# Layer one's gate and MLP scale by packed TensorE rows, its MLP shift by VectorE dot products, the input weights' low parts on VectorE

## The chip, the cores and the metric

One core of one Trainium2 chip runs the whole program. TensorE (PE) multiplies matrices into PSUM, VectorE (DVE), ScalarE (ACT) and GpSimd (POOL) work on tiles, and SyncE (SP) issues nearly all transfers. The metric is device time of one execution in microseconds (us); the program is one launch.

## The reference

A two-layer generator: each layer turns a conditioning vector into six modulation vectors of 1024 (shift, scale and gate of the mixer, then shift, scale and gate of the MLP), for latent tokens (512) and context tokens (256) apart.

```python
for l in range(DEPTH):
    mx = jnp.split((silu_c @ w_mod[l] + b_mod[l])[:, None, :], N_MOD, axis=-1)
    mc = jnp.split(silu_cc @ w_mod[l] + b_mod[l], N_MOD, axis=-1)
    zx = modulate(rms_norm(x, norm1_g[l]), mx[0], mx[1]) @ w_in[l]
    zc = modulate(rms_norm(ctx, norm1_g[l]), mc[0], mc[1]) @ w_in[l]
    ...                                        # Fourier, latent attention, convolution
    x = x + mx[2] * mixer_rest(fx, gx, attn_x, l)
    hx = modulate(rms_norm(x, norm2_g[l]), mx[3], mx[4])
    x = x + mx[5] * channel_mlp(hx, l)
return rms_norm(x, final_norm_g)
```

What matters here is where the 6144 modulation columns of layer one (l = 0 in the code) are made, and when each is needed: mx[0] and mx[1] at once, mx[2] (the gate, columns 16 to 23 of the tile mod, 128 values to a column) at the output projection, mx[3] and mx[4] (columns 24 to 39) at the norm before the MLP.

## The kernel before

Activations lie transposed: features on the 128 partitions, tokens along the row. Every product is made in three passes (mm3): a float32 operand is split into a rounded high part and a low part that is the rest, and high x high, high x low and low x high are summed in PSUM. load_w does it for weights: SP loads 512 KB into a tile raw, ScalarE writes the high part, and the engine named by eng (GpSimd by default) subtracts it from raw for the low part.

In start, the input projection of layer one runs over eight blocks of 128 features. For each, load_win loads 896 columns of weights (tiles wk and hl, L152 the low part), and put_h makes the activations: VectorE scales (L345), ScalarE adds the shift and rounds (L346), VectorE makes the low part (L347). Shift and scale come from TensorE in four pieces: load_mod loads 512 columns of the modulation weights (four tiles mq), mod_rows multiplies them, eight matmuls whose stationary tile c32 has only 32 columns and which stand in four column groups of the array (tile_position, L324), and mod_cols turns the rows into columns with a small selection matrix sel4. sq_ctx sums the squares of the context tokens: ScalarE squares, GpSimd adds (L353).

In mixer, a convolution on VectorE (L747) and a Fourier part lead to attention, a loop over 48 units of a head and 128 queries. From its thirteenth unit on, every sixth puts one of four gate pieces into the background: gate_columns loads 256 columns (gw, 1 MB), multiplies them with cpp, which has two columns, and turns the result.

Then the output projection: eight blocks of weights wo, each 48 matmuls (the last two 24 at first, the context's 24 later), and behind each update adds the product into the residual on VectorE (L990) and squares it (ScalarE) into a sum for the norm. mod_group makes one column of mod by VectorE dot products (L270): it loads 128 transposed columns (mw, 512 KB) and multiplies and sums over 1024, once for latent and once for context. Sixteen columns, 24 to 39, are made here, behind the first blocks. At the end set_a and norm_chain start the MLP's norm (L216, L220, L221), and first_pairs splits the first MLP weights (hs, L1054 and L1055).

The order in which instructions stand on each engine is made by a scheduler from the program's order; each engine then runs its own list in that order, and SP's list is also the order of the loads. The scheduler also decides which buffer of a pool a load takes.

```python
wo_mods = [24, 32, 25, 33, 26, 34, 27, 35, 28, 36, 29, 37, 30, 38, 31, 39]
...
            for _ in range(3 if m < NW else 1):
                if wo_mods:
                    w = mwp.tile([P, D], F32, tag="mw", name=nm("mw"), bufs=4)
                    mod_group(mods, w, 0, wo_mods.pop(0))
```

## Time and profile before

| | us |
|---|---|
| median of 3 runs | 1632.77 |
| lowest, highest | 1628.58, 1635.89 |
| the profiled execution | 1634.36 |
| its span | 1632.6 |

| engine | busy us | share of the span |
|---|---|---|
| PE | 1520.0 | 93% |
| DVE | 1233.2 | 76% |
| ACT | 698.3 | 43% |
| POOL | 689.1 | 42% |

The program runs through stages with different limits, so these shares say little of one stage. Three stages hold what the change touches: the input projection (0 to 100 us), attention (about 165 to 352) and the output projection (about 352 to 430). The rest, the MLP of layer one and all of layer two, is issued in the same order before and after. In the rows below a line that begins with a start and a length names the engine behind them; in square brackets stands how long the engine was idle before and what ended that.

### The profile page before, as it was taken

What the parts mean: (1) busy time and instruction counts of PE and PEld (TensorE: products, weight loads), DVE (VectorE), ACT (ScalarE), POOL (GpSimd) and SP (SyncE); (2) the same over time, 40 slices, a digit from 0 to 9 for tenths busy, and PEclk for the clock granted to TensorE, in tenths of its full rate; (3) what the DMA queues carried; (4) which work ended last, traced back from release to release, by engine and by line L of the source; (5) the groups of instructions that cost most, each with busy time, mean ns of one, the idle gap of its engine ahead of it and who ended that gap; (6) DMA issues with size and microseconds to landing.
All of it is one profiled execution on the core that took longest, in us unless ns stands there. A gap on an engine that the chain in (4) does not pass through costs nothing.

```text
span 1632.6 us, 24752 instructions
## 1 busy us (share of the span) xinstructions
PE 1520.0 (93%) x9508; PEld 1329.1 (81%) x9508; DVE 1233.2 (76%) x1984; ACT 698.3 (43%) x1291; POOL 689.1 (42%) x455
## 2 busy tenths in 40 slices
PE   5898999999899999999999999899999979999997
PEld 3598877787788988889999988777878778889897
DVE  3379687779999799987887768978866676566655
ACT  3343577651432333323332244258954434444442
POOL 1415233213135455534444333343325566666671
PEclk9999999999899999999999999999999989999998
DMA  8321102147142333333433332100123122233322
GB/s 282 117 98 57 36 21 86 37 154 250 61 168 67 107 112 117 104 129 125 148 117 105 127 104 99 46 26 8 53 65 117 52 85 91 84 102 104 104 78 65
DMA packets 50567, 159.55 MB, mean 98 GB/s; under 512 B 5745, under 2 KB 13713, under 8 KB 49425
## 3 DMA queue, kind: packets, MB, share of 16 engines
q1 hardware_dynamic: 50016, 152.69, 28.6%
q0 software_dynamic: 432, 5.28, 0.8%
q8 instruction: 75, 1.23, 0.3%
q14 instruction: 44, 0.35, 0.1%
HBM read 155.84 MB, written 2.11 MB: 97 GB/s over the span
## 4 chain that ended last, share of the span: by engine, by line
PE 44%; DVE 30%; DMA 9%; issue 8%; ACT 6%; POOL 3%; SPq 0%; DVEq 0%; ACTq 0%; POOLq 0%
PE ps L156 23%; PE pv L156 10%; DVE mj L270 7%; DMA acc<-in_wmodT 7%; PE tr L156 5%; DVE aw L747 3%; DVE resx L990 2%; PE tr L865 2%; PE po L156 1%; ACT p L849 1%; PE p L156 1%; DVE t L1168 1%; DMA raw<-in_w 1%; DVE resc L990 1%; DVE t L1138 1%
## 5 line engine op out<-in xcount | busy, mean ns | idle before, releaser
L156 PE MATMUL ps<-y,hl 128*128 128x512 f32 (+1 forms) x2004 | 411.2, 358 | 13.0 <-DVE resc L990 4.7
L156 PEld LDWEIGHTS ps<-y,hl 128*128 128x128 f32 x2004 | 328.0, 190 | 74.3 <-DVE resc L990 8.8
L152 POOL TENSOR_TENSOR hl<-raw,hl 128x1024 fp32r<-128x1024 f32 (+2 forms) x92 | 229.8, 2500 | 271.1 <-ACT hl L151 263.1
L156 PE MATMUL pv<-y,hl 128*128 128x512 f32 (+1 forms) x1032 | 212.8, 356 | 5.7 <-POOL hl L152 2.7
L156 PEld LDWEIGHTS pv<-y,hl 128*128 128x128 f32 x1032 | 168.6, 189 | 37.4 <-POOL hl L152 3.2
L151 ACT ACTIVATE hl<-raw 128x1024 fp32r<-128x1024 f32 (+2 forms) x94 | 98.1, 1044 | 226.4 <-PE pv L156 112.0
L1055 POOL TENSOR_TENSOR hs<-raw,hs 128x512 fp32r<-128x512 f32 x95 | 133.2, 1404 | 125.6 <-ACT hs L1054 125.6
L156 PE MATMUL ps<-h,hs 128*128 128x256 f32 (+1 forms) x1080 | 151.2, 292 | 5.3 <-DVE t L1210 3.2
L156 PEld LDWEIGHTS ps<-h,hs 128*128 128x128 f32 x1080 | 140.1, 192 | 11.4 <-issue 3.6
L1054 ACT ACTIVATE hs<-raw 128x512 fp32r<-128x512 f32 x133 | 83.0, 629 | 146.8 <-PE tr L156 30.0
L270 DVE CUSTOM_DVE_ANT_0 mj<-acc,cb,vec 128x1024 bf16<-128x1024 f32 x64 | 103.1, 1611 | 39.7 <-DMA acc<-in_wmodT 39.7
L990 DVE SCALAR_TENSOR_TENSOR resx<-ps,mod,resx 128x512 f32<-128x512 f32 (+1 forms) x134 | 95.7, 719 | 40.2 <-PE ps L156 40.1
L1162 POOL TENSOR_TENSOR y<-t,y 128x256 fp32r<-128x256 f32 (+1 forms) x78 | 73.7, 959 | 120.2 <-DVE t L1168 112.8
L156 PE MATMUL tr<-h,hs 128*128 128x256 f32 x624 | 83.3, 283 | 0.0
L869 DVE TENSOR_TENSOR pT<-tr,pT 128x384 fp32r<-128x384 f32 (+1 forms) x144 | 74.1, 534 | 10.0 <-ACT pT L868 9.4
L868 ACT ACTIVATE pT<-tr 128x384 fp32r<-128x384 f32 (+1 forms) x144 | 65.9, 477 | 32.7 <-PE tr L865 31.7
L156 PE MATMUL pv<-h,hs 128*128 128x256 f32 (+1 forms) x504 | 77.2, 303 | 2.2 <-DVE h L221 2.2
L156 PEld LDWEIGHTS tr<-h,hs 128*128 128x128 f32 x624 | 78.5, 191 | 0.6
L865 PE MATMUL tr<-ident,p 128*128 128x128 f32 x416 | 68.7, 279 | 9.6 <-DVE pT L869 6.8
L156 PEld LDWEIGHTS pv<-h,hs 128*128 128x128 f32 x504 | 69.4, 194 | 5.9 <-DVE h L221 2.6
L156 PE MATMUL po<-pT,v 128*128 128x256 f32 x416 | 72.4, 298 | 1.3 <-DVE t L894 1.1
L1167 ACT ACTIVATE t<-t 128x256 f32<-128x256 f32 (+1 forms) x52 | 32.7, 629 | 93.7 <-DVE t L1210 93.7
(291 smaller groups left out, 2962.0 us busy)
## 6 DMA issues: line engine op xcount, KB each, us to landing
raw<-in_w SPq DMA_DIRECT2D x128, 512.0 KB, 3.7
acc<-in_wmodT SPq DMA_DIRECT2D x48, 512.0 KB, 3.5
raw<-in_wo SPq DMA_DIRECT2D x17, 512.0 KB, 4.3
mq<-in_wmods SPq DMA_DIRECT2D x16, 512.0 KB, 7.9
mw<-in_wmodT SPq DMA_DIRECT2D x16, 512.0 KB, 4.3
ztab<-in_dftx POOLq DMA_DIRECT2D x2, 2064.0 KB, 9.4
gw<-in_wmodg SPq DMA_DIRECT2D x4, 1024.0 KB, 4.9
y<-in_wmodT SPq DMA_DIRECT2D x8, 512.0 KB, 5.4
```

Of the source, the lines that this page charges most:

```text
L151: SC.activation(w[:, 0], raw, AF.Copy)
L152: side[eng].tensor_tensor(w[:, 1], raw, f(w[:, 0]), ALU.subtract)
L156: PE.matmul(o, lhsT=l, rhs=r, start=start, stop=stop)
L270: V.tensor_tensor_reduce(j, w, c[:, v], 1.0, vc("bmod", l, g), ALU.mult, ALU.add, mod[l][v][:, g:g + 1])
L747: V.scalar_tensor_tensor(acw[ct], us[ct][:, i:i + wide], vc("wdw", l, ct * TAPS + i), acw[ct], ALU.mult, ALU.add)
L865: PE.transpose(tr[:, (kt - ka) * P:(kt - ka + 1) * P], ptiles[i][:, kt * P:kt * P + P], ident)
L868: SC.activation(d[:, 0], src, AF.Copy)
L869: V.tensor_tensor(d[:, 1], src, f(d[:, 0]), ALU.subtract)
L990: mark[0] = V.scalar_tensor_tensor(r, pt[:, a - o0:b - o0], mod[l][v][:, gate * 8 + m:gate * 8 + m + 1], r, ALU.mult, ALU.add).ins
L1054: SC.activation(w[:, 0], src, AF.Copy)
L1055: side[eng].tensor_tensor(w[:, 1], src, f(w[:, 0]), ALU.subtract)
L1162: GP.tensor_tensor(ht[:, 1, a:a + n], src, f(ht[:, 0, a:a + n]), ALU.subtract)
```

## The change

The helpers load_mod, mod_rows and mod_cols move out of start and serve three places. The array wmods holds ten pieces of 512 columns instead of four; wmodg, with the gate's four pieces of 256, is gone. The gate (pieces 4 and 5) is made in attention and the MLP's scale (pieces 8 and 9) in the output projection, by packed TensorE rows; the MLP's shift (columns 24 to 31) stays with VectorE's dot products, now spread over the blocks by a table. load_win asks for the low parts on VectorE, and sq_ctx adds its squares there too. c32 and sel4 become constants of the whole program. Bytes loaded stay the same.

```diff
+    c32 = cst.tile([P, KT, 32], F32, name="c32")
+    sel4 = cst.tile([P, 2], F32, name="sel4")
...
+    def load_mod(q, pl, bufs):
+        ws = [pl.tile([P, 2, 512], F32, tag="mq", name=nm("mq"), bufs=bufs) for _ in range(4)]
+        for i, w in enumerate(ws):
+            SY.dma_start(w, A["wmods"][q, :, 2 * i:2 * i + 2])
+        return ws
+
+    def mod_rows(ws, pl, bufs):
+        pt = pst()
+        for k in range(KT):
+            g = 32 * (k % 4)
+            PE.matmul(pt[g:g + 32, :], lhsT=c32[:, k], rhs=ws[k // 2][:, k % 2], start=k < 4, stop=k >= 4,
+                      tile_position=(0, g))
+        r = pl.tile([P, 512], F32, tag="mr", name=nm("mr"), bufs=bufs)
+        SC.activation(r, pt, AF.Copy)
+        return r
+
+    def mod_cols(q, row):
+        pt = pst()
+        for i in range(4):
+            mm(pt[:, 2 * i:2 * i + 2], row[:, i * P:(i + 1) * P], sel4, True, True)
+        for v in range(2):
+            if q >= 4:
+                o = slice(4 * q, 4 * q + 4)
+                V.tensor_tensor(mod[0][v][:, o], pt[:, v:8:2], vc("bmod", 0)[:, o], ALU.add)
+                continue
...
         def load_win(k):
-            wks.append(load_w(A["win0"][k], 896, *((wk, "wk", 6) if k < 6 else ())))
+            wks.append(load_w(A["win0"][k], 896, *((wk, "wk", 6) if k < 6 else ()), eng="V"))
...
         def sq_ctx(kk):
-            sq = acc[:, S:T] if kk == 0 else tmp(C)
-            SC.activation(sq, xt[kk][:, S:T], AF.Square)
-            if kk:
-                GP.tensor_tensor(acc[:, S:T], acc[:, S:T], sq, ALU.add)
+            add_square(acc[:, S:T], xt[kk][:, S:T], kk == 0)
...
-        gp, pieces = [], list(range(4))
+        gp, pieces = [], [4, 5]
 
         def gate_columns(q):
-            w = gp[0].tile([P, KT, 256], F32, tag="gw", name=nm("gw"), bufs=1)
-            SY.dma_start(w, A["wmodg"][q])
-            yield 1
-            pt = pst()
-            for k in range(KT):
-                mm(pt[0:2, 0:256], cpp[:, k], w[:, k], k == 0, k == KT - 1)
-            rows = gp[0].tile([2, 256], F32, tag="gr", name=nm("gr"), bufs=1)
-            SC.activation(rows, pt[0:2, 0:256], AF.Copy)
-            yield 1
...
+            ws = load_mod(q, gp[0], 4)
+            yield 1
+            row = mod_rows(ws, gp[0], 1)
+            yield 1
+            mod_cols(q, row)
             yield 1
...
-        wo_mods = [24, 32, 25, 33, 26, 34, 27, 35, 28, 36, 29, 37, 30, 38, 31, 39]
+        wo_mods = {1: 8, 4: 9} if mods else {}
+        wo_dots = (2, 2, 1, 1, 1, 1, 0, 0) if mods else (0,) * KT
+        ready, dots = load_mod(8, mwp, 4) if mods else None, list(range(24, 32))
+        cols_of = []
...
-            if mods:
-                for _ in range(3 if m < NW else 1):
-                    if wo_mods:
-                        w = mwp.tile([P, D], F32, tag="mw", name=nm("mw"), bufs=4)
-                        mod_group(mods, w, 0, wo_mods.pop(0))
+            if cols_of:
+                mod_cols(*cols_of.pop())
+            if m in wo_mods:
+                q = wo_mods[m]
+                cols_of.append((q, mod_rows(ready, mwp, 2)))
+                if q < 9:
+                    ready = load_mod(q + 1, mwp, 4)
+            for _ in range(wo_dots[m]):
+                mod_group(mods, mwp.tile([P, D], F32, tag="mw", name=nm("mw"), bufs=2), 0, dots.pop(0))
```

How that moves instructions is shown at three places. The first is VectorE near the end of the input projection, where the last shift and scale columns arrive (tr_485) and the activations of the last two blocks (y) are made from x. Before:

```order
L337 TENSOR_TENSOR mod_79<-tr_485,vec 128x2 x2
L337 TENSOR_TENSOR mod_80<-tr_485,vec 128x2
L338 SCALAR_TENSOR_TENSOR av_83<-mod_79,vec 128x2
L337 TENSOR_TENSOR mod_80<-tr_485,vec 128x2
L345 SCALAR_TENSOR_TENSOR t_496<-x_122,av_83,bcs 128x512
L338 SCALAR_TENSOR_TENSOR av_84<-mod_80,vec 128x2
L345 SCALAR_TENSOR_TENSOR t_500<-x_123,av_83,bcs 128x512
L347 SCALAR_TENSOR_TENSOR y_99<-t_496,mod_79,y_99 128x512
```

After, from the row behind the first two of these columns on:

```order
L156 TENSOR_TENSOR hl_456<-raw_454,hl_456 128x896
L308 SCALAR_TENSOR_TENSOR av_85<-mod_81,vec 128x2
L306 TENSOR_TENSOR mod_82<-tr_485,vec 128x2
L352 SCALAR_TENSOR_TENSOR t_496<-x_123,av_85,bcs 128x512
L156 TENSOR_TENSOR hl_461<-raw_459,hl_461 128x896
L308 SCALAR_TENSOR_TENSOR av_86<-mod_82,vec 128x2
L354 SCALAR_TENSOR_TENSOR y_101<-t_496,mod_81,y_101 128x512
L352 SCALAR_TENSOR_TENSOR t_500<-x_124,av_85,bcs 128x512
L194 TENSOR_TENSOR sq_125<-sq_125,t_504 128x256
```

The two low parts of the weights (hl) and the additions of squares (sq) now stand between them; two more additions, the last y and one more addition follow. The first two blocks have the same form: both subtractions stand ahead of the two y.

The second is TensorE in the output projection, at the border between the second block of weights (product pv) and the third (product ps). Before:

```order
L156 MATMUL pv_3597<-y_3252,hl_3511 128x256 x2
L156 MATMUL pv_3597<-y_3252,hl_3511 128x512
L156 MATMUL pv_3597<-y_3252,hl_3511 128x256
L156 MATMUL ps_3676<-y_1360,hl_3671 128x512 x2
L156 MATMUL ps_3676<-y_1360,hl_3671 128x256 x2
L156 MATMUL ps_3676<-y_1360,hl_3671 128x512
```

After, where the rows tr are made from the four tiles of the MLP scale's first piece:

```order
L160 MATMUL pv_3580<-y_3232,hl_3491 128x512
L160 MATMUL pv_3580<-y_3232,hl_3491 128x256
L288 MATMUL tr_3637<-mq_3509,c_79 32x512 x2
L288 MATMUL tr_3637<-mq_3510,c_79 32x512 x2
L288 MATMUL tr_3637<-mq_3511,c_79 32x512 x2
L288 MATMUL tr_3637<-mq_3512,c_79 32x512 x2
L160 MATMUL ps_3673<-y_1360,hl_3668 128x512 x2
L160 MATMUL ps_3673<-y_1360,hl_3668 128x256 x2
```

The eight packed matmuls stand together between two blocks; the second piece stands in the same form between the fifth and the sixth, and each piece's columns one block later. On SP's list the four loads of the second piece and two loads of dot-product weights now stand ahead of the weights of the fifth block. In attention a piece's eight matmuls stand together too.

The third is ScalarE at the end of the output projection, where hl is the last block's weights, t the squares, hs the first MLP weights and t<-resx_3492 (before) and t<-resx_3472 (after) the last square that the norm needs. Before:

```order
L151 ACTIVATE hl_4013<-raw_4011 128x1024
L189 ACTIVATE t_3963<-resx_3490 128x512
L1054 ACTIVATE hs_4376<-raw_4374 128x512
L189 ACTIVATE t_3967<-resc_3501 128x256
L1054 ACTIVATE hs_4379<-raw_4374 128x512
L189 ACTIVATE t_4008<-resx_3491 128x512
L994 ACTIVATE t_4044<-resx_3492 128x512
L151 ACTIVATE hl_4175<-raw_4173 128x1024
```

After:

```order
L155 ACTIVATE hl_4005<-raw_4003 128x1024
L193 ACTIVATE t_3948<-resx_3470 128x512
L193 ACTIVATE t_3952<-resc_3481 128x256
L1055 ACTIVATE hs_4368<-raw_4366 128x512
L1055 ACTIVATE hs_4371<-raw_4366 128x512
L193 ACTIVATE t_4000<-resx_3471 128x512
L1055 ACTIVATE hs_4376<-raw_4374 128x512
L1055 ACTIVATE hs_4379<-raw_4374 128x512
L987 ACTIVATE t_4036<-resx_3472 128x512
L155 ACTIVATE hl_4167<-raw_4165 128x1024
```

Four copies hs instead of two now stand ahead of the last square; the second tile (raw_4374 after) is loaded into the buffer of the first (raw_4366) and waits for VectorE to be done with that.

## Rows read from the trace of the kernel before

**Rows 1.** Page, chain that ended last: share of the span by engine.

```profile
PE 44%; DVE 30%; DMA 9%; issue 8%; ACT 6%; POOL 3%; SPq 0%; DVEq 0%; ACTq 0%; POOLq 0%
```

**Rows 2.** Timeline: start us, us, engine, line, op, out<-in, count [idle before <-releaser].

```profile
22.24 2.07 POOL L152 TENSOR_TENSOR wk<-raw,wk 128x896 fp32r<-128x896 f32 x1 [6.06 <-ACT wk L151]
...
22.73 1.60 DVE L338 SCALAR_TENSOR_TENSOR av<-mod,vec 128x2 f32<-128x2 f32 x1
...
25.99 1.20 PE L156 MATMUL ps<-y,wk 128*128 128x512 f32 x2 [3.56 <-ACT y L346]
...
52.59 0.16 DVE L338 SCALAR_TENSOR_TENSOR av<-mod,vec 128x2 f32<-128x2 f32 x1
```

**Rows 3.** Timeline, tail of the input projection, VectorE and TensorE.

```profile
68.33 0.29 DVE L337 TENSOR_TENSOR mod<-tr,vec 128x2 f32<-128x2 f32 x3 [12.52 <-PE tr L156]
...
73.05 0.40 PE L156 MATMUL ps<-y,hl 128*128 128x512 f32 x1
...
77.75 1.01 PE L156 MATMUL tr<-ones,sq 128*128 128x2 f32 x4 [2.55 <-POOL sq L353]
...
80.67 3.66 PE L156 MATMUL ps<-y,hl 128*128 128x512 f32 x8
...
89.74 1.56 PE L156 MATMUL pv<-y,hl 128*128 128x512 f32 x6
...
91.14 2.30 PE L156 MATMUL tr<-y,wk 128*128 128x256 f32 x18
```

**Rows 4.** Stretches: us, busy PE, PEld, DVE, ACT, POOL, PEclk, DMA share, GB/s.

```profile
80.00:84.00 4.00, 4.00 (x12) 3.32 (x13) 2.47 (x7) 1.69 (x4) 0.00 (x0) 0.50 0.00 0
```

**Rows 5.** Groups by form: line engine op names shapes xcount | busy, mean ns.

```profile
L897 DVE TENSOR_TENSOR y<-t,y 128x768 fp32r<-128x768 f32 x1 | 1.0, 959 | 0.9 <-ACT y L896 0.9
```

**Rows 6.** Chain in order of time: start us, us without overlap, what.

```profile
35.74 0.98 PE tr L324 x4
...
37.85 0.79 PE tr L156 x8
...
43.09 0.99 PE tr L324 x8
...
302.67 3.54 PE tr L156 x16
...
309.64 0.53 PE tr L156 x4
```

**Rows 7.** Stretches of attention, with the gate pieces and behind them.

```profile
236.00:312.00 76.00, 73.06 (x460) 56.49 (x460) 55.96 (x127) 53.94 (x116) 23.27 (x15) 1.00 0.22 72
...
312.00:352.00 40.00, 36.45 (x248) 31.18 (x247) 33.68 (x75) 28.83 (x68) 6.37 (x4) 1.00 0.13 41
```

**Rows 8.** Stretches of the output projection: most of it, and one moment.

```profile
355.00:404.00 49.00, 48.77 (x269) 41.83 (x267) 44.14 (x62) 10.00 (x15) 13.71 (x5) 1.00 0.80 269
...
362.00:364.00 2.00, 2.00 (x14) 1.73 (x13) 1.93 (x5) 0.00 (x0) 0.00 (x0) 1.00 0.32 121
```

**Rows 9.** Groups by form, output projection: the dot products.

```profile
L270 DVE CUSTOM_DVE_ANT_0 mj<-mw,cb,vec 128x1024 bf16<-128x1024 f32 x32 | 50.5, 1579 | 4.0 <-DMA mw<-in_wmodT 3.7
```

**Rows 10.** Timeline, last block of the output projection and the norm behind it.

```profile
405.11 0.73 PE L156 MATMUL pv<-y,hl 128*128 128x512 f32 x2 [1.34 <-ACT hl L151]
...
408.58 6.81 PE L156 MATMUL pv<-y,hl 128*128 128x512 f32 x22 [2.74 <-POOL hl L152]
...
412.93 0.63 ACT L1054 ACTIVATE hs<-raw 128x512 fp32r<-128x512 f32 x1 [1.92 <-DMA raw<-in_w]
...
415.23 3.00 PE L156 MATMUL ps<-y,hl 128*128 128x256 f32 x24
...
421.55 0.38 PE L156 MATMUL tr<-ones,t 128*128 128x2 f32 x2 [2.21 <-ACT t L994]
...
424.17 5.16 PE L156 MATMUL ps<-y,hl 128*128 128x256 f32 x24
...
430.32 2.06 DVE L216 SCALAR_TENSOR_TENSOR t<-resx,av,tr 128x512 f32<-128x512 f32 x3 [0.46 <-PE tr L156]
```

More of the change, by code (lines that the diff above doesn't have):

```diff
@@ L270, in mod_group @@
             V.tensor_tensor_reduce(j, w, c[:, v], 1.0, vc("bmod", l, g), ALU.mult, ALU.add, mod[l][v][:, g:g + 1])
+    def load_mod(q, pl, bufs):
[21 more added lines that the diff above has]
+                continue
+            for i in range(2):
+                o = slice(8 * i + 2 * q, 8 * i + 2 * q + 2)
+                V.tensor_tensor(mod[0][v][:, o], pt[:, 4 * i + v:4 * i + 4:2], vc("bmod", 0)[:, o], ALU.add)
+            g = slice(2 * q, 2 * q + 2)
+            V.scalar_tensor_tensor(av[0][v][:, g], mod[0][v][:, 8 + 2 * q:10 + 2 * q], 1.0, vc("g1", 0)[:, g],
+                                   ALU.add, ALU.mult)
     def start(h):
@@ L278, in start @@
         SY.dma_start(cpp, A["cpp"])
-        c32 = ws.tile([P, KT, 32], F32, name="c32")
         V.memset(c32, 0.0)
@@ L298, in start @@
         SY.dma_start(srow.rearrange("o v (a p) -> (o v a) p", p=P), cr)
-        sel4 = x0.tile([P, 2], F32, name="sel4")
         V.tensor_reduce(sel4, ident.rearrange("p (j v) -> p v j", v=32)[:, 0:2, :], AX.X, ALU.add)
@@ L308, in start @@
         wks, wq, rows = [], {}, {}
-        def load_mod(q):
-            wq[q] = [ws.tile([P, 2, 512], F32, tag="mq", name=nm("mq"), bufs=8) for _ in range(4)]
-            for i, w in enumerate(wq[q]):
-                SY.dma_start(w, A["wmods"][q, :, 2 * i:2 * i + 2])
         def load_win(k):
-            wks.append(load_w(A["win0"][k], 896, *((wk, "wk", 6) if k < 6 else ())))
-        def mod_rows(q):
-            pt = pst()
-            for k in range(KT):
-                g = 32 * (k % 4)
-                PE.matmul(pt[g:g + 32, :], lhsT=c32[:, k], rhs=wq[q][k // 2][:, k % 2], start=k < 4, stop=k >= 4,
-                          tile_position=(0, g))
-            rows[q] = ws.tile([P, 512], F32, tag="mr", name=nm("mr"), bufs=2)
-            SC.activation(rows[q], pt, AF.Copy)
-        def mod_cols(q):
-            pt = pst()
-            for i in range(4):
-                mm(pt[:, 2 * i:2 * i + 2], rows[q][:, i * P:(i + 1) * P], sel4, True, True)
-            g = slice(2 * q, 2 * q + 2)
-            for v in range(2):
-                for i in range(2):
-                    o = slice(8 * i + 2 * q, 8 * i + 2 * q + 2)
-                    V.tensor_tensor(mod[0][v][:, o], pt[:, 4 * i + v:4 * i + 4:2], vc("bmod", 0)[:, o], ALU.add)
-                V.scalar_tensor_tensor(av[0][v][:, g], mod[0][v][:, 8 + 2 * q:10 + 2 * q], 1.0, vc("g1", 0)[:, g],
-                                       ALU.add, ALU.mult)
+            wks.append(load_w(A["win0"][k], 896, *((wk, "wk", 6) if k < 6 else ()), eng="V"))
         def put_h(k, v):
@@ L369, in start @@
                 if k % 2 == 0:
-                    mod_rows(q)
+                    rows[q] = mod_rows(wq[q], ws, 2)
                     load_win(k + 2)
@@ L373, in start @@
                     if q + 1 < 4:
-                        load_mod(q + 1)
+                        wq[q + 1] = load_mod(q + 1, ws, 8)
             w = wks[k]
@@ L379, in start @@
             if k % 2 == 0 and q < 4:
-                mod_cols(q)
+                mod_cols(q, rows[q])
                 for i in range(2):
```

20 lines of the change are left out of this document (6 added, 14 removed).

## The prediction

> **What bounds the kernel now.** I read the chain that ended last first: TensorE holds 44% of it, VectorE 30%, GpSimd 3%, DMA 9% [rows 1]. So work on TensorE costs time nearly everywhere, work on VectorE in some stages, and GpSimd matters only where somebody waits for it. Then I read the three places that the change touches, each by its timeline and its table of stretches, and looked at which wait ends last there.
>
> At the start (0 to 100 us) TensorE multiplies the input weights. GpSimd's subtractions make the low parts, and they cost more than their own time: the tiny VectorE instruction av takes 0.16 us at 52.59, but 1.60 us at 22.73, where it ends together with a GpSimd subtraction that began at 22.24; the first weight matmul waits at 25.99 for what comes behind it [rows 2]. Later TensorE waits 2.55 us at 77.75 for GpSimd's sum of squares, and the eight matmuls at 80.67 take 3.66 us [rows 3] because the granted clock in 80 to 84 is 0.50, the lower of its two levels, 1.2 GHz, after those waits [rows 4].
>
> In attention (236 to 312 us, the stretch with the four gate pieces) TensorE is busy 73.06 of 76.00 us, VectorE 55.96 and ScalarE 53.94; in the 40 us behind it, without gate pieces, TensorE is busy 36.45 [rows 7].
>
> In the output projection (from 355 us) TensorE is busy 48.77 of 49.00 us up to 404 [rows 8], and only then does VectorE's backlog bite: the sums for the norm start at 421.55 after waiting 2.21 us for ScalarE, and the norm itself begins at 430.32 [rows 10].
>
> **Start: low parts and squares go to VectorE.** Eight subtractions of 896 columns leave GpSimd. VectorE does 768 columns in 0.959 us [rows 5], so 896 take about 0.959 x 896 / 768 = 1.12 us, 9 us in all; seven additions of 256 columns follow, by the same row about 0.35 us each. Most of it lies beside TensorE's work. Two gains are on the path.
>
> First, the av at 22.73 falls from 1.60 to about 0.16 us: -1.4 us for the first weight matmul. Against it, the order puts two subtractions (2.24 us) ahead of the first low activation. TensorE has three high matmuls, a packed pair and one more high matmul to do meanwhile, about 3 us at the start's clock, so I take no loss; if the second weight tile comes only as late as before, this gain is gone (bound 0).
>
> Second, the tail of the input projection. From 73.05 to 91.14 TensorE does 42 matmuls of 512 columns and two small groups. At (91.14 - 89.74) / 6 = 0.233 us each [rows 3] and 0.8 us a group (the small x8 group at 37.85 [rows 6]) that is 9.8 + 1.6 = 11.4 us of work in 18.1 us: 6.7 us lost to waits and the low clock. Now VectorE does it all. From 68.33, when the shift and scale columns arrive [rows 3], it has two subtractions (2.24), four additions (1.4), four passes at 2.06 / 3 = 0.69 (2.8) [rows 10] and 0.6 us of small ones: 7.0 us, to 75.3 or a little later. TensorE reaches the sums after ten matmuls, at 73.05 + 2.3 = 75.4. I take 0.5 us of wait there and 0.6 us for the root on GpSimd: -6.7 + 1.1 = -5.6 us. If the clock still falls, the eight matmuls and their neighbours lose about 2.5 us again: -3.1. What follows is VectorE's convolution, which starts when TensorE ends this part, so the gain is carried on.
>
> Start: **-7.0 us** (-3 to -7.5).
>
> **Attention: four pieces of 256 gate columns become two of 512.** A piece before costs TensorE 3.54 us for its rows and 0.53 for its columns [rows 6]; four are 16.3 us. The new form runs at the start of the kernel already: a packed block of two matmuls takes 0.98 us, a block of four 0.99, and the columns 0.79 [rows 6]. In the new order a piece's eight matmuls stand together, two blocks of four, so 2.0 + 0.8 = 2.8 us, with margin 2.9; two pieces are 5.8 us. That takes 10.5 us off TensorE, 73.06 to 62.6 us. Not all comes through, since softmax on ScalarE and VectorE is close behind. The next stretch shows the rate without pieces: TensorE busy 36.45 of 40, 91% [rows 7]. 62.6 / 0.911 = 68.7 us instead of 76: **-7.3 us**. The ends: -10.5 if all comes through; -3.4 if every pair pays the 0.98 alone (two pieces 2 x (3.9 + 0.8) = 9.4 us, and (73.06 - 6.9) / 0.911 = 72.6). ScalarE's copies, two large ones for four small ones, are hidden.
>
> **Output projection: half of the dot products go, two pieces come.** VectorE's 32 dot products take 50.5 us [rows 9]; 16 go, -25 us of VectorE. TensorE gets 2 x 2.9 = 5.8 us, and here nothing covers that: it is busy 48.77 of 49.00. The transfer for the first piece takes the place in the queue of the four dot-product weights, as many bytes; by 362 to 364 the DMA share is down to 0.32 [rows 8]. TensorE does five full blocks and a half one of 5.6 us from 355 to 403.8, so 8.6 us a block, and needs the piece behind the first of them, at about 364; I cost that wait at nothing (bound +2).
>
> What goes: the last block's matmuls waited 1.34 us for ScalarE and 2.74 for GpSimd and then ran slowly [rows 10], since ScalarE's copy of its weights stood behind squares that waited for VectorE. From 405.11 - 1.34 = 403.8 to 408.58 + 6.81 = 415.4 that is 11.6 us for 24 x 0.233 = 5.6 us of work: a stall of 6.0 us, which pays for the 5.8. The last block ends near 415, as before. VectorE's update then follows at once instead of 5 us late, so the squares could go to TensorE at about 416 instead of 421.55. But the order shows what is late next: two copies hs of the next weights now stand on ScalarE ahead of that last square, and their transfer starts only when VectorE is done with the tile before it. Of that tile before, GpSimd freed the buffer at about 408.5 and the first copy began at 412.93, 4.4 us later [rows 10]. Now, from the same 408.5 or a microsecond earlier: 4.4, two copies of 0.63 (1.3), a subtraction (0.7), 4.4 again, two copies and the square (1.9), 12.7 us, to 420 or 421. So about 1 us is left of 5.5. The 24 matmuls behind take 5.16 us at 424.17 where the same ones took 3.00 at 415.23 [rows 10]; with a shorter wait those 2.2 us may come back. I take **-2.5 us** (-6 to +2).
>
> **Sum.** -7.0 - 7.3 - 2.5 = -16.8 us against the profiled execution's 1634.36 us (its span is 1632.6): 1617.6. The median of the runs is 1.6 us lower, 1632.77, which makes 1616.0. The ends of the terms: -3 - 3.4 + 2 = -4.4 us (1628) and -7.5 - 10.5 - 6 = -24 us (1609).
>
> **Rivals.**
> Cover gone (22%): attention runs at VectorE's and ScalarE's pace once the pieces are thin, and the late hs copies eat the whole gain of the projection. For it: the two are 74% and 71% busy in that stretch. Against it: the stretch behind still has TensorE at 91%. Start alone and -2 of attention: -9 us, 1624.
>
> Packing doesn't pay (12%): a packed block among full-width ones stops TensorE's stream at both its borders, so that four thin blocks cost 0.98 each. For it: two matmuls cost as much as four [rows 6]. Against it: the new order keeps a piece together. -7 - 3.4 and in the projection 2 x 4.7 - 5.8 = 3.6 us of TensorE more, so its -2.5 becomes +1: -9.4 us, 1623. The Trainium skill, TensorEngine Tiling (Array Packing), Key Properties, has such a rule against the change: switching the tiling mode drains TensorE. By that rule the trace agrees that a border costs something, since 0.98 for two and 0.99 for four leaves most of the 0.98 to it.
>
> Slower (6%): the projection starves. On SP's queue the weights of the fifth output block now stand behind the second piece's four loads, which wait for TensorE, and two dot-product loads, which wait for VectorE; DMA is at a share of 0.80 already [rows 8]. If that block and the ones behind it come late, each may cost what the last block cost before, 6.0 us. After three such blocks the gain of 16.8 us is gone; there are four, 24 us, which gives +7 us, 1640. Against it: TensorE is past the first piece at about 364 + 2.0 = 366, and VectorE through four dot products of 1.6 us [rows 9] and four short updates at about 374, so the weights are issued then; they are needed two blocks, a piece and 364 later, 364 + 2.9 + 2 x 8.6 = 384.
>
> **How the numbers follow.** The forecast has 60%: **1616 us**. Cover gone 22%, packing 12%, slower 6%. The range 1607 to 1629 takes in the ends of the terms and both rivals that stay faster, and leaves out the slower one. A measurement of this kernel can tell about 0.5%, 8 us, from no change: under 1624.6 is faster. The forecast, half of cover gone and most of packing: 0.80 faster; the rest of those and a starved projection that only eats the gain: 0.16 same; 0.04 slower.
>
> **What would show it.** Start: av near 0.16 us at its first place, no wait of TensorE over 1 us at the sums, a clock of 1.00 where it was 0.50, and the convolution 7 us earlier. Attention: pieces of about 2.0 + 0.8 us, the stretch some 7 us shorter. Projection: no wait of the last block, TensorE's sums waiting for a ScalarE square behind hs copies, the norm 2 to 3 us nearer to the projection's start. I am wrong if TensorE waits for weights in the projection, if the packed blocks cost near 1 us a pair, or if attention keeps its length.

## Result, and the profile after

The changed kernel takes 1613.13 us, the median of 4 runs (1610.79 to 1615.65), beside 1634.33 (1628.58 to 1639.95) for the kernel before: a ratio of 0.9873, 95% interval 0.9848 to 0.9899. The forecast was 1616.0 us with a range of 1607 to 1629. It is faster by 1.3%, and the size was close: 1634.33 x (1 - 0.9873) = 20.8 us gained where 16.8 were forecast. The profiled execution took 1613.05 us, its span 1611.3.

The chain that ended last, share of the span by engine, has moved from VectorE and DMA towards TensorE (to be read beside [rows 1]):

```profile
PE 57%; DVE 22%; issue 6%; ACT 5%; DMA 5%; POOL 3%; DVEq 0%; SPq 0%; POOLq 0%; ACTq 0%
```

**Start.** The timeline of the changed kernel (start us, us, engine, line, operation, count, and in brackets the idle time before and what ended it), TensorE and VectorE, first at the place of [rows 2], then at that of [rows 3]:

```profile
17.82 3.55 PE L288 MATMUL tr<-mq,c 128*32 128x512 f32 x16
...
23.48 0.16 DVE L308 SCALAR_TENSOR_TENSOR av<-mod,vec 128x2 f32<-128x2 f32 x1
...
25.30 1.22 PE L160 MATMUL ps<-y,wk 128*128 128x512 f32 x2 [2.12 <-ACT y L353]
...
68.25 1.08 DVE L156 TENSOR_TENSOR hl<-raw,hl 128x896 fp32r<-128x896 f32 x1
...
72.78 2.50 PE L160 MATMUL ps<-y,hl 128*128 128x512 f32 x10
75.13 0.58 PE L160 MATMUL tr<-ones,sq 128*128 128x2 f32 x4
75.57 0.71 PE L160 MATMUL ps<-y,hl 128*128 128x512 f32 x2
76.74 0.71 PE L160 MATMUL tr<-ident,sm 128*128 128x128 f32 x4 [0.46 <-POOL sm L179]
...
84.29 2.32 PE L160 MATMUL tr<-y,wk 128*128 128x256 f32 x18
```

av takes 0.16 us at its first place instead of 1.60; the sums (75.13) wait for nothing instead of 2.55 us; the tail from 72.78 to 84.29 takes 11.5 us instead of 18.1. The clock stays up where it had fallen [rows 4] (the stretch: us, busy PE, PEld, DVE, ACT, POOL, granted clock, DMA share, GB/s):

```profile
80.00:84.00 4.00, 4.00 (x19) 3.23 (x18) 3.54 (x9) 2.21 (x6) 0.00 (x0) 1.00 0.01 2
```

Between these two executions little of the lead at the first weight matmul is left where the tail begins (72.78 against 73.05). That matmul waited 2.12 us for its activation instead of the 3.56 in [rows 2], 1.44 less, as forecast. But the packed rows ahead of it took 3.55 us, where they had taken 2.38, and the granted clock from 25 to 30 us was 0.50 (0.66 before). The length of these rows is scatter, not the edit: over the fourteen profiles below it goes from 2.38 to 3.64 us, and gate_only, which has the old start, has 3.64. The kernel before, then gate_only:

```profile
18.24 2.38 PE L324 MATMUL tr<-mq,c 128*32 128x512 f32 x16
```

```profile
18.13 3.64 PE L288 MATMUL tr<-mq,c 128*32 128x512 f32 x16
```

TensorE shows no wait inside them. The median of their records is 1.06 us in the changed kernel and in gate_only, 0.62 in the kernel before; why is open. The lead has to be read from the means of several kernels, which stand in the part on the prediction.

**Attention.** One of the two gate pieces on TensorE (to be read beside [rows 6], where a piece of half the size took 3.54 and 0.53):

```profile
233.56 1.92 PE L288 MATMUL tr<-mq,c 128*32 128x512 f32 x16
235.42 0.86 PE L160 MATMUL ps<-kE,q 128*128 128x256 f32 x4
...
239.11 0.95 PE L160 MATMUL tr<-sel,mr 128*128 128x2 f32 x8
239.92 0.53 PE L858 MATMUL tr<-ident,p 128*128 128x128 f32 x3
```

From start to start it takes 1.86 + 0.81 = 2.67 us. TensorE over the whole stage, between the second and third of the marks defined below (the stretch as in [rows 4]), in the kernel before, then in the changed one:

```profile
235.47:355.62 120.15, 113.66 (x729) 91.41 (x730) 91.55 (x203) 83.84 (x185) 30.16 (x18) 1.00 0.21 69
```

```profile
229.97:342.54 112.57, 103.80 (x698) 86.78 (x699) 90.55 (x199) 82.75 (x183) 30.41 (x18) 1.00 0.19 63
```

TensorE is busy for 9.9 us less, and the stage is 7.6 us shorter: 2.3 us of the difference became idle time.

**Output projection.** TensorE from the first full block to the norm, then the norm's first pass on VectorE (to be read beside [rows 10]):

```profile
342.54 8.59 PE L160 MATMUL pv<-y,hl 128*128 128x512 f32 x48
351.06 1.92 PE L288 MATMUL tr<-mq,c 128*32 128x512 f32 x16
352.91 8.70 PE L160 MATMUL ps<-y,hl 128*128 128x512 f32 x48
...
396.20 5.76 PE L160 MATMUL pv<-y,hl 128*128 128x512 f32 x24
401.81 3.04 PE L160 MATMUL ps<-y,hl 128*128 128x256 f32 x24
...
404.82 0.36 PE L160 MATMUL tr<-ones,t 128*128 128x2 f32 x2
...
406.39 3.12 PE L160 MATMUL ps<-y,hl 128*128 128x256 f32 x24
...
410.49 2.06 DVE L220 SCALAR_TENSOR_TENSOR t<-resx,av,tr 128x512 f32<-128x512 f32 x3 [0.46 <-PE tr L160]
```

TensorE waits for nothing: not at the last block (396.20), not at the sums (404.82), and the 24 matmuls behind them take 3.12 us instead of 5.16. Their granted clock is 1.00 now (406.4 to 409.4); before it was about half of that:

```profile
424.00:429.00 5.00, 5.00 (x25) 5.00 (x26) 2.29 (x5) 0.42 (x1) 2.26 (x2) 0.52 0.37 111
```

The copies hs on ScalarE that I feared ahead of the last square come just in time: the square ends at 403.96, and TensorE gets to it at 404.82 (SP's issue of the copies' transfers, then ScalarE):

```profile
393.53 5.71 SPq L1061 DMA_DIRECT2D raw<-in_w  x2
```

```profile
389.96 1.06 ACT L155 ACTIVATE hl<-raw 128x1024 fp32r<-128x1024 f32 x1 [3.30 <-PE ps L160]
...
396.93 1.16 ACT L1055 ACTIVATE hs<-raw 128x512 fp32r<-128x512 f32 x2 [5.08 <-DMA raw<-in_w]
...
402.28 1.15 ACT L1055 ACTIVATE hs<-raw 128x512 fp32r<-128x512 f32 x2 [3.68 <-DMA raw<-in_w]
403.34 0.62 ACT L987 ACTIVATE t<-resx 128x512 f32<-128x512 f32 x1
```

### The profile page after: what moved, and what is told of

It is laid out like the page before. It is cut to its first block, busy times and chain, and to the rows that moved or that the text cites. A ratio compares the mean times of both kernels' runs of the same rounds, so it can differ in the third digit from the quotient of the medians.

```text
span 1611.3 us, 24743 instructions
## 1 busy us (share of the span) xinstructions
PE 1512.9 (94%) x9524; PEld 1322.3 (82%) x9524; DVE 1210.0 (75%) x1967; ACT 697.9 (43%) x1291; POOL 663.3 (41%) x440
## 4 chain that ended last, share of the span: by engine, by line
PE 57%; DVE 22%; issue 6%; ACT 5%; DMA 5%; POOL 3%; DVEq 0%; SPq 0%; POOLq 0%; ACTq 0%
PE ps L160 30%; PE pv L160 15%; PE tr L160 6%; DVE mj L274 4%; DMA acc<-in_wmodT 3%; DVE aw L751 2%; ACT p L842 2%; DVE ac L751 2%; DVE resx L983 2%; PE tr L858 2%; PE po L160 1%; POOL hl L156 1%; PE tr L288 1%; PE p L160 1%; DVE t L1139 1%
## 5 line engine op out<-in xcount | busy, mean ns | idle before, releaser
L156 POOL TENSOR_TENSOR hl<-raw,hl 128x1024 fp32r<-128x1024 f32 (+1 forms) x90 | 223.4, 2483 | 252.2 <-ACT hl L155 252.1
L179 POOL TENSOR_TENSOR sm<-sm,mhalf 128x2 f32<-128x2 f32 (+2 forms) x16 | 17.7, 1109 | 193.8 <-DVE sm L177 193.8
L983 DVE SCALAR_TENSOR_TENSOR resx<-pv,mod,resx 128x512 f32<-128x512 f32 (+1 forms) x75 | 54.0, 722 | 34.1 <-PE pv L160 33.9
```

What stands on the lines that cost most here:

```text
L156: side[eng].tensor_tensor(w[:, 1], raw, f(w[:, 0]), ALU.subtract)
L983: mark[0] = V.scalar_tensor_tensor(r, pt[:, a - o0:b - o0], mod[l][v][:, gate * 8 + m:gate * 8 + m + 1], r, ALU.mult, ALU.add).ins
```

## A ruler for the experiments: lengths of stages

The time of one kernel scatters by 5 us (four executions of the changed kernel) to 21 us (23 executions of the kernel before in one session), as much as one part of the change is worth or more, so I read every run's profile at four marks on the path: the matmuls of the context tokens behind the tail of the input projection (91.14 before, [rows 3]); the transposes that wait 2 us for VectorE's sm, shortly ahead of the first gate piece; the first full block of the output projection; the norm's first pass (430.32 before, [rows 10]). The second and third mark in the trace of the kernel before:

```profile
235.47 0.52 PE L865 MATMUL tr<-ident,p 128*128 128x128 f32 x3 [2.03 <-DVE sm L850]
...
355.62 8.64 PE L156 MATMUL pv<-y,hl 128*128 128x512 f32 x48
```

Lengths in us between the marks (rest: from the norm to the end of the span), then the median time and its ratio to the kernel before on the same chip (whose median lay between 1634.3 and 1636.5 in the four sessions, so ratios are compared, not medians):

| run | start | to attention | attention | projection | rest | median | ratio, 95% interval |
|---|---|---|---|---|---|---|---|
| before | 91.14 | 144.33 | 120.15 | 74.70 | 1202.3 | 1634.33 | 1 |
| after | 84.29 | 145.68 | 112.57 | 67.95 | 1200.8 | 1613.13 | 0.9873, 0.9848 to 0.9899 |
| after_again | 83.14 | 147.47 | 114.11 | 68.40 | 1202.9 | 1616.48 | 0.9870, 0.9847 to 0.9893 |
| start_only | 83.20 | 145.16 | 120.15 | 74.57 | 1204.6 | 1628.71 | 0.9954, 0.9936 to 0.9972 |
| low_only | 85.20 | 144.71 | 120.17 | 71.91 | 1205.9 | 1632.22 | 0.9962, 0.9941 to 0.9983 |
| squares_only | 90.35 | 144.46 | 120.21 | 74.26 | 1207.3 | 1636.61 | 0.9987, 0.9964 to 1.0010 |
| gate_only | 91.74 | 145.70 | 112.50 | 72.76 | 1206.3 | 1629.73 | 0.9964, 0.9946 to 0.9983 |
| proj_only | 91.61 | 144.33 | 120.19 | 67.92 | 1203.4 | 1629.45 | 0.9961, 0.9944 to 0.9978 |
| dots_late | 84.48 | 145.82 | 113.45 | 71.25 | 1202.5 | 1616.55 | 0.9860, 0.9825 to 0.9894 |
| twice | 84.61 | 145.85 | 112.52 | 71.38 | 1202.5 | 1617.61 | 0.9861, 0.9826 to 0.9896 |
| gate_twice | 84.78 | 145.66 | 116.34 | 68.42 | 1207.1 | 1617.41 | 0.9869, 0.9837 to 0.9902 |
| scale_early | 83.26 | 146.57 | 119.90 | 63.31 | 1202.5 | 1618.65 | 0.9897, 0.9868 to 0.9925 |
| one_piece | 83.17 | 144.26 | 113.38 | 69.25 | 1204.6 | 1618.13 | 0.9879, 0.9856 to 0.9902 |
| shift_too | 84.38 | 145.76 | 113.36 | 73.60 | 1196.9 | 1615.59 | 0.9867, 0.9843 to 0.9892 |

The five runs with the old attention agree within 0.06 us there (120.15 to 120.21), the seven with the changed attention within 1.6 us (112.50 to 114.11, mean 113.1). The projection as before takes 71.91 to 74.70 us (five runs, mean 73.6), as after 67.92 to 68.42 (four runs, mean 68.2). The rest, in which nothing was changed, takes 1196.9 to 1207.3 us. A difference of 3 us can be told here in attention and in the projection as after, but not in the time of the whole.

The scatter in attention goes with the granted clock. The three kernels in which it stays at 1.00 (after, gate_only, twice) take 112.50 to 112.57 us; the other four have a stretch of 4 or 5 us with a mean of 0.57 to 0.66 (0.57 from 231 to 235 us in after_again, 0.66 from 276 to 281 in dots_late) and take 113.36 to 114.11. What made the clock fall there I have not tested.

## Experiments

**Each part alone.** start_only is the kernel before with the two edits of the start:

```diff
-            wks.append(load_w(A["win0"][k], 896, *((wk, "wk", 6) if k < 6 else ())))
+            wks.append(load_w(A["win0"][k], 896, *((wk, "wk", 6) if k < 6 else ()), eng="V"))
...
-                GP.tensor_tensor(acc[:, S:T], acc[:, S:T], sq, ALU.add)
+            add_square(acc[:, S:T], xt[kk][:, S:T], kk == 0)
```

> The kernel before with only the low parts of the input weights and the additions of squares moved from GpSimd to VectorE; gate and MLP modulation as before. My theory (three separate gains that add up): TensorE's input projection ends about 6.5 to 7 us earlier, nothing else changes, so 7 us less in all, ratio 0.9957, attention and the output projection of the same length as before. Rival (the gains only count together, because a stage that starts earlier gives the lead back, as the lead of 6.9 us in the changed kernel had shrunk to 5.5 us by 214 us): 3 us or less remain, ratio 0.998 or more.

gate_only has only the gate's pieces changed, proj_only only the projection's table:

```diff
-        gp, pieces = [], list(range(4))
+        gp, pieces = [], [4, 5]
...
```

> The kernel before with only the gate as two packed pieces in attention; start and output projection as before. My theory: the stretch from the thirteenth unit to the end of attention is 7.5 us shorter, the projection is unchanged with its stall at the last block, so 7.5 us less, ratio 0.9954. Rival (attention goes at the pace of softmax on VectorE and ScalarE once the pieces are thin): 2 to 4 us less, ratio 0.998, with longer waits of TensorE for pT and p.

```diff
-        wo_mods = [24, 32, 25, 33, 26, 34, 27, 35, 28, 36, 29, 37, 30, 38, 31, 39]
+        wo_mods = {1: 8, 4: 9} if mods else {}
+        wo_dots = (2, 2, 1, 1, 1, 1, 0, 0) if mods else (0,) * KT
...
```

> The kernel before with only the output projection changed: the MLP scale as two packed pieces on TensorE, eight dot-product columns instead of sixteen. My theory: TensorE does 5.3 us more, the last block's stall of 6 us, the wait for the last square and the low clock behind it go, so from the start of the projection to the norm 6.7 us less, ratio 0.9959. Rival (the gain of 6.7 us in the changed kernel came from the earlier gate and start, through transfers that had more time): 0 to 3 us less, ratio 0.998 to 1.000, with a wait of the last block or of the sums.

Measured: 0.9954, 0.9964 and 0.9961. Their product is 0.9880, the changed kernel's ratio 0.9873 and 0.9870. In each the stage that was touched is shorter (start 83.20, attention 112.50, projection 67.92), and the others keep their length within the scatter of the table. So the parts add up, and all three rivals fall: those of start_only and proj_only by the ratios already, that of gate_only (0.998, which its interval takes in) by the 7.7 us that attention is shorter. Ahead of attention the kernels with the changed start take about 1 us more (145.8 as the mean of nine, 144.26 to 147.47; 144.8 of three without, 144.33 to 145.70). That too goes with the granted clock: in the changed kernel it was 0.83 from 205 to 215 us where the same work before (212 to 222) had 1.00. All fourteen profiles have a stretch of low clock between 113 and 130 us; eight of the nine have a further one near 155 or 210 us, and one_piece, which has not, takes 144.26. But gate_only has one with the old start (145.70). I have not tested why it falls, so that it is the start's doing is not shown.

**Which edit of the start.** low_only moves only the subtractions, squares_only only the additions (each one of the two edits above).

> The kernel before with only the low parts of the input weights moved from GpSimd to VectorE; GpSimd still adds the squares. My theory (the root of the late tail is GpSimd's subtraction, beside which VectorE's small av took 1.50 and 2.07 us instead of 0.16, and behind which the activations, the squares and the additions came late): without them the squares are ready about 1 us earlier, TensorE's wait of 2.55 us at the sums falls to about 1 us, and if the clock then stays up 4 to 6 us of start_only's 7.2 come: ratio about 0.997. Rival (the additions on GpSimd, which the wait is put down to, are the cost): the wait stays above 2 us and the gain is under 2 us, ratio 0.999.

> The kernel before with only the additions of squares moved from GpSimd to VectorE; GpSimd still makes the low parts. My theory: av stays at 1.5 to 2.1 us beside the subtractions, the activations and squares come as late as before, three additions of 0.35 us on VectorE replace 2.51 us on GpSimd, so the sums wait about 1.2 us instead of 2.55; the gain is 1 to 3 us, ratio 0.999. Rival (the additions on GpSimd were the cost): nearly all of start_only's 7.2 us, ratio 0.996.

Measured: the start is 6.3 us shorter with the subtractions moved (85.20 against 91.50, the mean of the three runs with the old start) and 1.2 us with the additions moved (90.35); the time of squares_only (0.9964 to 1.0010) can't tell its 1.2 us from nothing. My theories hold, and both rivals fall. Timeline of low_only, then of squares_only, at the tail:

```profile
68.91 0.15 DVE L338 SCALAR_TENSOR_TENSOR av<-mod,vec 128x2 f32<-128x2 f32 x1
...
75.34 0.61 PE L156 MATMUL tr<-ones,sq 128*128 128x2 f32 x4 [1.13 <-POOL sq L353]
```

```profile
69.78 4.21 POOL L152 TENSOR_TENSOR hl<-raw,hl 128x896 fp32r<-128x896 f32 x2 [7.64 <-ACT hl L151]
...
70.16 0.29 DVE L337 TENSOR_TENSOR mod<-tr,vec 128x2 f32<-128x2 f32 x3 [7.75 <-PE tr L156]
70.42 1.50 DVE L338 SCALAR_TENSOR_TENSOR av<-mod,vec 128x2 f32<-128x2 f32 x1
...
71.96 2.57 DVE L345 SCALAR_TENSOR_TENSOR t<-x,av,bcs 128x512 f32<-128x512 f32 x1
...
78.46 0.58 PE L156 MATMUL tr<-ones,sq 128*128 128x2 f32 x4 [0.95 <-DVE sq L190]
```

With GpSimd's subtractions still there, VectorE's av takes 1.50 us and the scaling behind it 2.57 instead of 0.75, and the squares are late whoever adds them; the stretch from 80 to 84 us has a clock of 0.57. Without them av takes 0.15 us, the additions on GpSimd cost a wait of 1.13 us, and the clock is 1.00 (the stretch in squares_only, then in low_only):

```profile
80.00:84.00 4.00, 3.93 (x12) 3.30 (x13) 2.35 (x6) 1.69 (x4) 0.02 (x1) 0.57 0.00 0
```

```profile
80.00:84.00 4.00, 4.00 (x19) 3.25 (x18) 3.85 (x10) 1.87 (x6) 0.00 (x0) 1.00 0.00 0
```

The wait that the profile of before puts down to the additions, "[2.55 <-POOL sq L353]", was made mostly by the subtractions several steps earlier: they hold up av and the scaling on VectorE, behind which come the activations and then the squares on ScalarE, and only then the additions. That a subtraction holds them up is what the Trainium skill says on the page SBUF — State Buffer, Who interferes with whom: a VectorE instruction with two inputs in SBUF and a GpSimd instruction that reads SBUF contend for a port that they share, and the page calls that an exclusive lock. The trace agrees: three small additions of mod (70.16), one input of which lies in PSUM, take 0.29 us together beside a subtraction; av, with its inputs in SBUF, ends with the first subtraction (at 71.9), and the scaling, which takes 0.75 us alone, ends 0.5 us after the second (73.99).

**Late dot products.** dots_late keeps every instruction of the changed kernel and moves the eight dot-product columns behind the last four blocks:

```diff
-        wo_dots = (2, 2, 1, 1, 1, 1, 0, 0) if mods else (0,) * KT
+        wo_dots = (0, 0, 0, 0, 2, 2, 2, 2) if mods else (0,) * KT
```

> The changed kernel with the same eight dot-product columns placed behind the last four blocks (two behind each) instead of the first six; every instruction is the same. My theory (what the projection gained is that VectorE had no backlog when its last updates came): the updates of the last blocks and the last square come late again, TensorE's sums wait 2 to 5 us, the clock behind them falls, and the norm is 4 to 8 us later than in the changed kernel: about 1619 us. Rival (only the amount of work on each engine counts): no difference, 1613 us.

Measured: the projection takes 71.25 us instead of 68.2, 3.1 more; the time (ratio 0.9860) can't tell that. TensorE's timeline:

```profile
407.81 0.38 PE L160 MATMUL tr<-ones,t 128*128 128x2 f32 x2 [1.67 <-ACT t L987]
...
409.39 4.57 PE L160 MATMUL ps<-y,hl 128*128 128x256 f32 x24
```

The wait at the sums is back, and so is some of the low clock behind it. The granted clock from 409 to 413 us is 0.69. The mechanism is as I said, its size smaller: the wait is 1.67 us, not 2 to 5, and the projection 3.1 us longer, not 4 to 8.

**What a packed piece costs.** twice multiplies each piece of the projection a second time, gate_twice each piece of attention:

```diff
+                mod_rows(ready, mwp, 2)
                 cols_of.append((q, mod_rows(ready, mwp, 2)))
```

> The changed kernel with each packed piece of the MLP scale multiplied twice in the output projection (eight more packed matmuls behind the first eight, their result is not used). It prices a piece where TensorE never waits. My theory (a packed block of four costs 0.93 us, at borders and inside alike, and the path goes through TensorE): 3.7 us more to the norm, 1617 us. First rival (most of a piece's price is the change between packed and full-width matmuls, which the second eight do not pay again): under 2 us more. Second rival (the last square behind the copies of the next weights ends later than TensorE anyway): nothing more.

```diff
+            mod_rows(ws, gp[0], 1)
             row = mod_rows(ws, gp[0], 1)
```

> The changed kernel with each of the two gate pieces in attention multiplied twice (the second result is used, the first is not). The second eight matmuls of a piece cost TensorE 1.72 us (from the run of the same kind in the output projection), 3.4 us for both. My theory (TensorE bounds this part of attention, so what a piece takes is paid in full): attention 3 to 4 us longer, about 1617 us. Rival (TensorE waits for softmax often enough to hide thin pieces): under 1.5 us.

Measured in the projection: 71.38 us instead of 68.2, 3.2 more, so both rivals fall. TensorE in twice (the profile has two records for each packed matmul):

```profile
351.50 3.64 PE L288 MATMUL tr<-mq,c 128*32 128x512 f32 x32
355.07 8.71 PE L160 MATMUL ps<-y,hl 128*128 128x512 f32 x48
```

Sixteen packed matmuls take 355.07 - 351.50 = 3.57 us, eight 352.91 - 351.06 = 1.85. So the second eight cost 1.72 us, and the two borders between packed and full-width work only 1.85 - 1.72 = 0.13 us. A rule that I had taken as a rival (the Trainium skill, TensorEngine Tiling (Array Packing), Key Properties: changing the tiling mode drains TensorE) is not refuted, but here it costs next to nothing.

In gate_twice the scheduler put one full-width matmul between the two eights of the first piece, and several with a wait of 0.49 us between those of the second, so each eight pay their own 1.85:

```profile
234.03 1.93 PE L288 MATMUL tr<-mq,c 128*32 128x512 f32 x16
235.88 0.39 PE L160 MATMUL ps<-kE,q 128*128 128x256 f32 x1
236.20 1.92 PE L288 MATMUL tr<-mq,c 128*32 128x512 f32 x16
```

The matmul between takes 236.20 - 235.88 = 0.32 us, where one of its size takes 3.04 / 24 = 0.13 in a row of its like (401.81 in the changed kernel): by that price the two borders cost 0.2 us.

Attention takes 116.34 us instead of 113.1: 3.2 more of the 3.7 added. It has a stretch of low clock too (0.62 from 280 to 284 us); beside the three kernels that have one at about the same place (113.36 to 113.45) it is 2.9 us longer. So most of it is paid, about 0.8 us is hidden, and the rival (under 1.5 us) falls.

**Other splits.** Three kernels divide the sixteen MLP columns in other ways: scale_early makes the scale in attention, one_piece gives half of the scale back to VectorE, shift_too makes everything on TensorE. after_again is the changed kernel beside them.

```diff
-        gp, pieces = [], [4, 5]
+        gp, pieces = [], [4, 5, 8, 9]
...
-        wo_mods = {1: 8, 4: 9} if mods else {}
+        wo_mods = {}
...
```

> The changed kernel with the two pieces of the MLP scale moved from the output projection, where TensorE never waits, into attention behind the two gate pieces (at the units that had gate pieces before); the projection keeps only the eight dot-product columns. My theory (a piece costs its 2.7 us in full where TensorE is always busy, and less where it waits for softmax: it is busy 32.75 of 38 us from 262 to 300 us): the projection gets 5.3 us shorter, attention 2 to 5 us longer, so 1 to 3 us less than the changed kernel, about 1611 us. Rival (the last square behind the copies of the next weights is the end that counts, as I forecast): the projection gains nothing, since the sums wait for that square, and attention gets longer: 2 to 5 us more than the changed kernel.

```diff
-        wo_mods = {1: 8, 4: 9} if mods else {}
-        wo_dots = (2, 2, 1, 1, 1, 1, 0, 0) if mods else (0,) * KT
+        wo_mods = {1: 8} if mods else {}
+        wo_dots = (3, 2, 2, 2, 2, 1, 0, 0) if mods else (0,) * KT
-        ready, dots = load_mod(8, mwp, 4) if mods else None, list(range(24, 32))
+        ready, dots = load_mod(8, mwp, 4) if mods else None, list(range(24, 32)) + list(range(36, 40))
...
```

> The changed kernel with only the first piece of the MLP scale on TensorE; the other four of its columns go back to VectorE's dot products (twelve instead of eight, spread 3, 2, 2, 2, 2, 1 over the first six blocks). My theory (TensorE's 2.7 us for a piece are on the path, VectorE's dot products cost nothing as long as no backlog is left at the last blocks): VectorE gets 8 x 1.6 = 12.8 us more and keeps up, the last square comes in time, so 1 to 2.7 us less than the changed kernel, about 1611 us. Rival (VectorE is close behind already, as when the same dot products stood at the last blocks): the updates come late again, TensorE's sums wait 2 us or more, no gain or up to 4 us more.

```diff
-        wo_mods = {1: 8, 4: 9} if mods else {}
-        wo_dots = (2, 2, 1, 1, 1, 1, 0, 0) if mods else (0,) * KT
+        wo_mods = {1: 6, 2: 7, 4: 8, 5: 9} if mods else {}
+        wo_dots = (0,) * KT if mods else (0,) * KT
...
```

> The changed kernel with the MLP shift on TensorE too: four packed pieces in the output projection, no dot products. My theory (TensorE is the only bound there by now, VectorE's remaining dot products are covered): two pieces more at 2.7 us each, so 5.3 us more than the changed kernel, about 1618 us. Rival (VectorE's dot products still delay the updates): less than 3 us more.

> The changed kernel once more, unchanged, so that it stands beside the variants of its projection and its attention on the same chip, with more runs. All theories: 1613 us, ratio 0.987.

scale_early: the projection is 4.9 us shorter (63.31), attention 6.8 us longer (119.90), for 2 x 2.67 = 5.3 us of work. I expected part of it to vanish in TensorE's idle time (32.75 of 38 us busy from 262 to 300 us); hardly any did, and my theory fell. Not all of the 6.8 us is the pieces', though: there are two stretches of low clock (0.57 from 230 to 234 us, 0.72 from 280 to 286). One at the first place is in after_again (114.11), one at the second in dots_late (113.45), 1.6 and 0.9 us above 112.5; by these, an estimate, 4.9 of the 5.3 us were paid. That a piece delays the transposes that softmax waits for, since TensorE works through its list in order, is a likely reason and not shown. In the projection the last square is late after all (TensorE):

```profile
407.35 0.38 PE L160 MATMUL tr<-ones,t 128*128 128x2 f32 x2 [1.14 <-ACT t L987]
```

one_piece: the projection takes 69.25 us, 1.1 more. TensorE has 2.7 us less to do there and gives it all back at the sums, since the last update on VectorE is late (TensorE and ScalarE):

```profile
402.85 0.38 PE L160 MATMUL tr<-ones,t 128*128 128x2 f32 x2 [2.60 <-ACT t L987]
...
404.68 4.39 PE L160 MATMUL ps<-y,hl 128*128 128x256 f32 x24
```

```profile
402.17 0.63 ACT L987 ACTIVATE t<-resx 128x512 f32<-128x512 f32 x1 [4.39 <-DVE resx L983]
```

My theory fell and the rival held: VectorE keeps up with eight columns behind the first six blocks, not with twelve.

shift_too: the projection takes 73.60 us, 5.4 more, as expected, with no wait anywhere (sums and the matmuls behind them):

```profile
411.43 0.36 PE L160 MATMUL tr<-ones,t 128*128 128x2 f32 x2
...
412.99 3.12 PE L160 MATMUL ps<-y,hl 128*128 128x256 f32 x24
```

Yet its time is that of the changed kernel (0.9867 beside 0.9870, each to about 0.0025, 4 us). In the profiled execution the 6.6 us by which the norm is later than in the changed kernel (417.10 against 410.49) still stand 43 us later (a stretch of matmuls that begins at 453.54 there begins at 460.18), but the rest as a whole is the shortest of all, 1196.9 us. All four of its executions took 1614.16 to 1617.65 us, like the five of after_again (1613.19 to 1617.81), so it is hardly chance of the one profiled; where the rest would gain is open. No split beat the changed kernel.

## Why the prediction was right, and where not

**Start, -7.0: measured -7.6** (83.9 as the mean of nine runs, 91.5 of three), of which about 1 us, by the means, is lost ahead of attention. Both halves came. The first (-1.4): av fell to 0.16 us, and the first weight matmul waits 2.12 or 2.13 us in all nine, 3.56 or 3.57 in the three. Where the tail begins (the first matmul with the last two weight blocks, hl, at 72.78 in the changed kernel) the means are 72.4 and 73.8, 1.4 us apart. That the two profiled executions are only 0.27 us apart there is chance: the packed rows, 2.38 us before and 3.55 after, scatter by as much, and the kernel before had the shortest of all. The second (-5.6) gave 6.2 by the means (11.5 us for the tail, where the three took 17.7) and 6.6 between the two executions: 11.5 us in all, where I had forecast 11.4 of work and 1.1 of waits; 0.46 us of it is the wait for the root (0.6), none for the sums (0.5), and the clock is 1.00. A subtraction takes 1.09 us (1.12), an addition 0.42 (0.35).

**Attention, -7.3: measured -7.0** (113.1 against 120.2). With the clock at 1.00 throughout it is -7.6 (112.5). A piece takes 2.67 us instead of the 2.9 I used. The step from TensorE's work to the time held: I had it busy 91% of the shorter stretch, and it is busy 103.80 of 112.57 us, 92%. So a part of the cover did go, as forecast. That all of it goes (cover gone, 22%: only 2 us of attention) is refuted by the 7.0 us, and by gate_twice and scale_early, in which most of an added piece is paid. Packing doesn't pay (12%) is refuted too; the step behind it, that most of the 0.98 us of a pair is the price of a border, was a misreading: both borders of a piece cost 0.13 to 0.2 us together. A pair stands in two of the four column groups and a block of four in all four; that both take one turn (0.98 us with borders, 1.72 / 2 = 0.86 without) fits groups that work side by side, but I have not tested it.

**Output projection, -2.5: measured -5.5** as a mean of runs (68.2 against 73.6), -6.75 between the two profiled executions. TensorE's own sum was right: the last block ends 401.81 - 342.54 = 59.3 us after the projection's start, before 415.23 - 355.62 = 59.6, so the two pieces and the stall do cancel. The step that failed, in its size, is the term for what is late next. I priced the chain of the copies hs at 12.7 us from a buffer free at 408.5 or a microsecond earlier, and left 1 us of 5.5. Counted from the projection's start, the buffer was free 1.9 us earlier (393.53 - 342.54 = 51.0 instead of 52.9), because GpSimd's subtraction for the last block took 2.40 us with no dot product beside it, not 3.40, and began 0.95 us sooner. Before, then after:

```profile
405.13 3.40 POOL L152 TENSOR_TENSOR hl<-raw,hl 128x1024 fp32r<-128x1024 f32 x1 [8.03 <-ACT hl L151]
```

```profile
391.10 2.40 POOL L156 TENSOR_TENSOR hl<-raw,hl 128x1024 fp32r<-128x1024 f32 x1 [7.65 <-ACT hl L155]
```

And the chain took 403.96 - 393.53 = 10.4 us: a transfer 3.4 instead of 4.4, two copies 1.06 instead of 1.3. Why the transfers were shorter is not shown; before, two loads of dot-product weights had been issued 5 us ahead of them. So TensorE finds the square ready, and the sums begin 3.65 us earlier, not 1. The clock that "may come back" came back (1.00, where 424 to 429 had 0.52): 2.04 us at the 24 matmuls, and 1.05 at the sums ahead of them, which I had not counted. 3.65 + 1.05 + 2.04 = 6.74.

**Sum.** By the means of stages -7.6 + 1.0 - 7.0 - 5.5 = -19.1 us, by the ratios -20.8 and -21.3. The forecast of -16.8 was short by the projection's term; between -19.1 and the ratios lie 2 us, less than the ratios' intervals (some 4 us each way). The starved projection (6%) did not show: TensorE never waits for weights in the changed kernel's projection.

## What to carry to other kernels

When TensorE waits for the last of a row of small instructions, look for what slowed the ones ahead of it: the releaser in the row (the additions) was worth 1.2 us, the engine beside it (GpSimd's subtractions) 6.3. A stall that disappears is worth the work that took its place only if the next late chain is priced too, and that chain is priced from rows in which it does not share an engine with what is removed: a GpSimd subtraction of 1024 columns at 2.4 us, not at the 3.40 that it takes behind a dot product. And where parts are worth 0.4% each, compare lengths of stages between marks on the path, over several kernels that share the stage, and look at the granted clock before a difference of 1 or 2 us is put down to an edit: the two executions compared first differ by 0.27 us where the means differ by 1.4. The time of the whole tells such a part from no change only with a dozen executions, and variants that differ by less not at all.

## What the runs showed of the hardware that I had not expected

A switch between packed and full-width matmuls costs about 0.13 us for both borders (0.2 by gate_twice), and eight packed matmuls of 32 columns by 512 take 1.72 us without them. VectorE's two-column av takes 0.15 us alone and up to 2.07 us beside a GpSimd subtraction of 896 columns. The cost comes back the other way, and one of the two pays: in the kernel before, GpSimd's subtraction of 1024 columns takes 3.40 us at 405.13, behind a dot product that began at 405.05; at 383.22 it takes 2.40, and the dot product that began with it (383.21) 3.49 instead of 1.28. Idle time of TensorE inside attention hid little of a piece that was put there: about 0.8 us of 3.7 in gate_twice, by an estimate 0.4 of 5.3 in scale_early. Attention's length is the same within 0.07 us (112.50 to 112.57) in three kernels with the granted clock at 1.00, and 0.8 to 1.6 us longer with one stretch of 4 to 5 us at 0.57 to 0.66.
